# Forming the block sums of the second round's left operands at the transposes, and keeping them in DRAM

## The chip, the core and the metric

The kernel runs on one core of one Trainium2 chip. The core has a matrix engine (TensorE, PE in the profile, with PEld for its weight loads), VectorE (DVE), ScalarE (ACT), GpSimd (POOL), and SyncE (SP), whose queue issues all DMAs of this kernel. The engines run their own instruction queues in order and wait for each other by semaphores. The metric is the time on the device, in microseconds, from the median of several runs; lower is better. Before the change it is 2823.95 us, the median of three runs between 2823.14 and 2828.58.

## What is computed

Two layers of a decoder over 2048 positions of width 1024, all in float32. The first ("even") layer has eight dense attention heads, the second ("odd") layer three groups of dilated sliding windows. The change touches the second layer's way in:

```python
def odd_layer(x, g_norm, w_in, g_q, g_k, w_out):
    h = rmsnorm(x, g_norm)
    proj = h @ w_in                       # (2048 x 1024) @ (1024 x 5120)
    q, k, v, gate = jnp.split(proj, split_points(ODD_SIZES), axis=-1)
    ...
    q = rmsnorm(groups(q), g_q)
    k = rmsnorm(groups(k), g_k)
    att = dilated_window_attention(q, k, groups(v))
    mixed = merge_heads(att) * jax.nn.silu(gate)
    return x + mixed @ w_out
```

Here x is the output of the first layer, which ends with its own product, `x + mixed @ w_out`.

## The kernel before

**Products.** A float32 product is made of three TensorE passes over operands split in a high and a low part (`split`, lines 73 to 86: ACT writes the high part, DVE or POOL the rest; `mm3`, lines 88 to 93). A panel is 1024 rows by 512 columns of a result. It is computed by Winograd's form of Strassen's method (`panel_steps`, lines 261 to 339) with seven products of half-size blocks in place of eight. The left side, 1024 rows by 1024, falls into L11, L12, L21 and L22, and the seven left operands are

    A11 = L11   A12 = L12   A22 = L22
    S1 = L21 + L22   S2 = S1 - L11   S3 = L11 - L21   S4 = L12 - S2

A product takes two halves of 24 matmuls each, and after each half the panel calls `tick` (line 292), which lets other work issue a step. A panel thus has 14 of these half products. The products come in the order of line 177, A11, S2, A12, S3, S1, A22, S4. Results leave PSUM through four "res" buffers. For q and k columns each result is squared, summed and scaled (`norms`, lines 117 to 125; lines 1014 to 1020), and every square takes a buffer of the tag "c", of which there are four.

**Rounds.** Each layer's way in runs in two rounds of 1024 rows. A round of the second layer has ten panels: q, k and v of each of three groups, and the gate at the end. The first two panels of a round are opened together (`two`, lines 958 to 969): both do A11 and A12 first, then the rest of one, then of the other. Seven left operands fill seven of the eight "big" buffers, so those of the next round can only be written one by one, as the last panel of the round, the gate panel, gives up its own. `panel` calls `after` behind each product for that, which advances `left(k, T, 1, B, False)` (lines 342 to 419, called at line 1187).

**Left operands.** The rows of the second layer's input x1 lie in DRAM. `transpose_to` (lines 153 to 163) takes a tile of 128 rows: load, norm, eight transposes on TensorE, ACT copies with the gain into two "c" buffers named te, and two stores of 256 KB into T (hT1 in DRAM, hT in the profile), which holds all 2048 columns. `staggered` keeps several tiles in flight. At line 990 the pace of these steps for the second round's rows is set to every fourth half product, and they run beside the first three panels of the first round; `tick.finish()` behind the third panel (line 1208) does what is left.

At the change of rounds `left` then loads blocks of T into "c" buffers (lp), 28 loads of 256 KB, some blocks twice or three times, forms S2, S3, S1 and S4 on DVE and POOL (the helper at line 345), S2, S3 and S4 partly out of the split A11, A12 and S2, and splits each result into the big buffers. The reader finds this arithmetic in the profile as L345, the splits as L81 (ACT) and L86 (DVE), the loads of lp as SPq L362.

**What runs beside it.** Attention units of the second layer are issued step by step by `beat` (lines 1192 to 1197), beginning behind the first v panel. A unit loads q, k and v, transposes on TensorE, and passes through ACT and DVE several times (L1122, L1128, L1137, L1149, L1154). Its buffers "ld", "q" and "pT" are two each; its rows use the tag "x" (three buffers), which the tiles xt of the transposes use too.

**Order.** The program is issued through a scheduler that orders each engine's queue by the order in which the program was written, the free buffers of each tag, and its own model of the durations. So a step that is issued at a later half product has a lower priority there, and a tag without a free buffer holds back whatever needs it.

Of the kernel before, what the change touches and what calls it, by code (L numbers as in the profile page):

```python
# [8 lines left out]
F32 = mybir.dt.float32  # L9
F32R = mybir.dt.float32r  # L10
BF = mybir.dt.bfloat16  # L11
AF = mybir.ActivationFunctionType  # L12
OP = mybir.AluOpType
# [4 lines left out]
P = 128  # L18
S = 2048
D = 1024  # L20
KT = D // P  # L21
CH = 512  # L22
# [14 lines left out]
class K:  # L37
# [114 lines left out]

    def transpose_to(self, T, src, t, gain):

        nc = self.nc
        x = self.w4([P, D], name="xt")
        nc.sync.dma_start(x, src[t * P:(t + 1) * P, :])
        yield
        self.normalise(x)
        yield  # L160
        self.transposed(x, gain, lambda z: self.c2([P, 4, P], name="te"),
                        lambda z, d: nc.sync.dma_start(T[:, z * 4:(z + 1) * 4, t * P:(t + 1) * P], d))

# [12 lines left out]
A11, A12, S2, S3, S1, A22, S4 = range(7)  # L176
ORDER = (A11, S2, A12, S3, S1, A22, S4)
FIRST = (A11, A12, S2, S3, S1, A22, S4)
# [77 lines left out]
def panel(*args, **kw):  # L256
    for _ in panel_steps(*args, **kw):
        pass
# [82 lines left out]

def left(k, T, r, A, staged=True):

    nc = k.nc
    tt = lambda o, a, b, op, e=None: (e or nc.vector).tensor_tensor(o, a, b, op=op)  # L345
    sub, plus = OP.subtract, OP.add

    A.extend([None] * 7)

    def new(j, name):  # L350
        A[j] = k.big([P, 4, 2, CH], F32R, name=name)
        return A[j]

    def put(t, kk, src):
        k.split(t[:, kk, 0], t[:, kk, 1], src, "act", "dve")

    tags = itertools.cycle(("ld", "q", "pT") if staged else ("c",))

    def piece(block, kk):
        c = k.c2(name="lp", tag=next(tags))  # L360
        t0 = r * ROUND + block * CH
        nc.sync.dma_start(c, T[:, kk, t0:t0 + CH])  # L362
        return c

    half = lambda t, kk: [t[:, kk, z].bitcast(F32) for z in range(2)]
    if staged:
        F = k.big([P, KT, CH], name="stage")
        for z in range(2):
            nc.sync.dma_start(F[:, z * 4:(z + 1) * 4], T[:, z * 4:(z + 1) * 4, r * ROUND:r * ROUND + CH])
    for z, name in enumerate(("A11", "A12")):  # L370
        t = new((A11, A12)[z], name)
        for kk in range(4):
            put(t, kk, F[:, z * 4 + kk] if staged else piece(0, z * 4 + kk))
        yield
    t = new(S2, "S2")
    for kk in range(4):
        l21, s = piece(1, kk), piece(1, 4 + kk)
        tt(s, l21, s, plus, nc.gpsimd if kk % 2 else None)
        if staged:
            tt(s, s, F[:, kk], sub)  # L380
            tt(F[:, 4 + kk], F[:, 4 + kk], s, sub, nc.gpsimd)
            tt(F[:, kk], F[:, kk], l21, sub, nc.gpsimd if kk % 2 else None)
        else:
            for h in half(A[A11], kk):
                tt(s, s, h, sub)
        put(t, kk, s)
    yield
    t = new(S3, "S3")
    for kk in range(4):
        if staged:  # L390
            s = F[:, kk]
        else:
            s = piece(1, kk)
            hi, lo = half(A[A11], kk)
            tt(s, hi, s, sub)
            tt(s, s, lo, plus)
        put(t, kk, s)
    yield
    yield
    t, t2 = new(S1, "S1"), new(A22, "A22")  # L400
    for kk in range(4):
        l21, s = piece(1, kk), piece(1, 4 + kk)
        tt(l21, l21, s, plus, nc.gpsimd if kk % 2 else None)
        put(t, kk, l21)
        put(t2, kk, s)
    yield
    t = new(S4, "S4")
    for kk in range(4):
        if staged:
            s = F[:, 4 + kk]  # L410
        else:
            s = k.c2(name="lp")
            hi, lo = half(A[A12], kk)
            h2, l2 = half(A[S2], kk)
            tt(s, hi, h2, sub)
            tt(s, s, lo, plus)
            tt(s, s, l2, sub)
        put(t, kk, s)
    yield


def left_direct(k, x, gain, A, spare):
# [171 lines left out]
def staggered(gens):  # L594

    gens, flight = iter(gens), []
    while True:
        flight = [g for g in flight if next(g, "end") != "end"]
        g = next(gens, None)
        if g is not None:  # L600
            next(g)
            flight.insert(0, g)
        elif not flight:
            return
        yield


def even_projection(k, x, w, first, first_left, early, late):
    tc, nc = k.tc, k.nc
    c2, dr = k.c2, k.dram  # L610
    k.fT = {n: dr.tile([P, 4, 2, S], F32R, name=f"f{n}T") for n in "qk"}
    k.sT = {n: dr.tile([P, 4, 2, S], F32R, name=f"s{n}T") for n in "qk"}
# [154 lines left out]
def even_attention(k, tail):  # L767
# [20 lines left out]
    def load_q(kind, h, u):  # L788
# [7 lines left out]
        return q  # L796

    def qk(kind, h, u, q, tile, left):

        kt, vt = heads[kind, h]  # L800
# [130 lines left out]
def odd_layer(k, x, x1, even_w_out, w_in, w_out, out):  # L931
    tc, nc = k.tc, k.nc
    c2, dr = k.c2, k.dram
    T = dr.tile([P, KT, S], F32, name="hT1")
    plain = lambda c0: [[(c0, 256)], [(c0 + 256, 256)]]
    outs = [(even_w_out, plain(n * CH)) for n in range(2)]
    rounds = [[(n, g) for g in gs for n in "qkv"] + [("gate", 0)] for gs in ((1, 0, 2), (2, 1, 0))]
# [2 lines left out]
                [2, 2] + [2, 1, 1, 1, 1, 1, 1, 1, 1] * 2)  # L940
    A = []
    lefts = left(k, k.mixT, 0, A)
    yield W, lefts

    tick = Pace()

    def residual(r, n):
        def emit(block, half, g, src):
            t0 = r * ROUND + block * CH + g * 256
            c0 = n * CH + half * 256  # L950
            view = lambda d: d[t0:t0 + 256, c0:c0 + 256].rearrange("(r p) c -> p r c", p=P)
            a = c2([P, 2, 256], name="x1t")
            nc.sync.dma_start(a, view(x))
            nc.vector.tensor_tensor(a, src.rearrange("p (r c) -> p r c", r=2), a, op=OP.add)
            nc.sync.dma_start(view(x1), a)
        return each(emit)

    def two(A, emits, tick, after=None):

        ps = [panel_steps(k, A, W, "t", emit, tick, after if n else None, first=("u", "x")[n])  # L960
              for n, emit in enumerate(emits)]
        for p in ps:
            next(p)
        yield
        for p in ps:
            next(p, None)
            yield

    for r in range(2):
        B = []  # L970
        nxt = left(k, k.mixT, 1, B) if r == 0 else left(k, T, 0, B)
        if r == 0:
            pace = Pace()
            pace.every = 2
            pace.add(lefts)
        both = two(A, [residual(r, n) for n in range(2)], pace if r == 0 else tick,
                   lambda j: None if j in EARLY else next(nxt))
        next(both)
        if r == 0:
            pace.finish()  # L980
            next(nxt)
            next(nxt)
        next(both)
        if r == 1:
            tick.finish()
            next(nxt)
            next(nxt)
        next(both)
        A = B
        tick.every = 1 if r == 0 else 4  # L990
        tick.add(iter("-"), staggered([k.transpose_to(T, x1, r * 8 + t, k.go) for t in (4, 5, 6, 7, 0, 1, 2, 3)]))

    qk = [dr.tile([S, 2, 2, HW], F32, name=f"qk{g}") for g in range(3)]
    vv = [dr.tile([S, 2, HW], F32, name=f"vv{g}") for g in range(3)]
# [189 lines left out]

    for r in range(2):
        B = []
        nxt = left(k, T, 1, B, False)
        for i, (name, grp) in enumerate(rounds[r]):
            rate = 3 if r == 0 or i < 3 else 1.3
            count = [0.0]  # L1190

            def beat():
                tick()
                count[0] += 1
                if count[0] >= rate:
                    count[0] -= rate
                    step()

            last = r == 0 and name == "gate"
            if i < 2:  # L1200
                if i == 0:
                    both = two(A, [emitter(r, *rounds[r][n]) for n in range(2)], beat)
                    next(both)
                next(both)
            else:
                panel(k, A, W, "t", emitter(r, name, grp), beat, (lambda j: next(nxt)) if last else None)
            if r == 0 and i == 2:
                tick.finish()
            if name == "v":
                nblk = S // GROUPS[grp][1] // P  # L1210
                if nblk == 1:
                    if r == 1:
                        queue.extend((True, attention(grp, hf, range(16), range(1))) for hf in range(2))
                else:
                    ns = range(r * nblk // 2, (r + 1) * nblk // 2)
                    queue.extend((False, attention(grp, hf, range(GROUPS[grp][1]), ns)) for hf in range(2))
        A = B
    ws = []
    for n in range(2):
        t = k.big([P, 4, 2, CH], F32R, name="wof")  # L1220
# [126 lines left out]
```

## Time and profile before

| | |
|---|---|
| median of three runs | 2823.95 us |
| profiled execution, its own time | 2826.53 us |
| its span, first to last instruction | 2824.8 us |
| busy share PE / DVE / ACT / POOL | 95% / 73% / 57% / 43% |
| mean granted TensorE clock | 0.979 |
| DMA moved | 449.43 MB, mean 159 GB/s |

The span is the profiled execution's time on the core; its own time is 1.7 us more, and 2.6 us above the median of the runs. A busy PE is not PE at its peak, since the ends of matmuls are modelled; the number of PE instructions in a stretch tells more. In lines of single instructions the columns are start, duration, engine, line, operation, what is written and read, and in square brackets the idle time before it and what ended that. In lines of groups the numbers are busy time and mean ns of one, then the idle time before them.

### The profile page before, as it was taken

Reading aid. Unit: us, or ns where it says so; the run is one execution under the profiler, and the core shown is the slowest. Engines: PE = TensorE matmul, PEld = TensorE weight load, DVE = VectorE, ACT = ScalarE, POOL = GpSimd, SP = SyncE. Lnnn points to the kernel's source line nnn. Section 1 sums busy time; section 2 is a strip of 40 time slices with the busy share of each in tenths; the row PEclk is TensorE's granted clock in tenths of the full one; section 3 lists DMA queues with packets and bytes.
Section 4 is the critical chain, followed back from the end, with each engine's and each line's share of the span. In section 5 each row is a group of like instructions: output and inputs, shape, how many; then the busy total and the mean of one; then the engine's idle time right before and its main releaser. Section 6 shows DMA issues by size and latency. Waiting matters only on the chain.

```text
span 2824.8 us, 55621 instructions
## 1 busy us (share of the span) xinstructions
PE 2676.4 (95%) x20191; PEld 2455.5 (87%) x20191; DVE 2052.7 (73%) x4373; ACT 1618.6 (57%) x3924; POOL 1223.4 (43%) x981
## 2 busy tenths in 40 slices
PE   6999999999999999998987999999989999999998
PEld 5898878998787789987887999999889999999876
DVE  7857684684888888888959857476797686763966
ACT  6465553454776666665364555555664577665642
POOL 3545464544544433326545544343245432422322
PEclk9999999999999999999998999999999999999999
DMA  5576544445433344435577553334543445444675
GB/s 180 181 222 210 172 160 154 154 142 192 144 111 118 112 123 144 139 104 173 187 232 246 154 179 107 121 122 146 169 128 126 139 140 166 132 147 134 219 254 183
DMA packets 398770, 449.43 MB, mean 159 GB/s; under 512 B 31712, under 2 KB 331040, under 8 KB 398496
## 3 DMA queue, kind: packets, MB, share of 16 engines
q1 hardware_dynamic: 398496, 445.89, 49.4%
q8 instruction: 159, 2.61, 0.4%
q14 instruction: 115, 0.94, 0.1%
HBM read 291.22 MB, written 154.57 MB: 158 GB/s over the span
## 4 chain that ended last, share of the span: by engine, by line
PE 62%; DVE 21%; DMA 7%; ACT 5%; issue 3%; POOL 1%; SPq 1%; DVEq 0%; ACTq 0%; POOLq 0%
PE ps L91 17%; PE ps L93 17%; PE ps L92 17%; DVE rest L828 4%; PE ps L863 2%; PE ps L1145 2%; DVE wop L86 2%; DVE A L86 2%; PE ps L1135 2%; PE ps L1116 2%; DVE lp L345 1%; DVE S L86 1%; PE ps L1061 1%; DVE pT L86 1%; DVE c L300 1%
## 5 line engine op out<-in xcount | busy, mean ns | idle before, releaser
L226 POOL TENSOR_TENSOR wraw<-wraw 128x512 f32<-128x512 f32 (+1 forms) x320 | 444.2, 1400 | 430.3 <-DVE wop L86 157.1
L81 ACT ACTIVATE wop<-wraw 128x512 fp32r<-128x512 f32 (+1 forms) x560 | 349.5, 629 | 383.4 <-PE ps L93 294.2
L86 POOL TENSOR_TENSOR wop<-wraw,wop 128x512 fp32r<-128x512 f32 (+1 forms) x240 | 329.4, 1375 | 534.0 <-ACT wop L81 503.8
L92 PE MATMUL ps<-wop,S 128*128 128x256 f32 (+1 forms) x1792 | 512.4, 286 | 18.1 <-DVE wop L86 16.8
L91 PE MATMUL ps<-wop,A 128*128 128x256 f32 (+1 forms) x1792 | 512.0, 287 | 14.2 <-DVE c L300 13.5
L91 PE MATMUL ps<-wop,S 128*128 128x256 f32 (+1 forms) x1792 | 515.8, 289 | 9.9 <-DVE c L300 6.3
L92 PE MATMUL ps<-wop,A 128*128 128x256 f32 (+1 forms) x1792 | 511.7, 286 | 2.2 <-DVE wop L86 1.5
L93 PE MATMUL ps<-wop,S 128*128 128x256 f32 (+1 forms) x1792 | 512.9, 287 | 0.0
L93 PE MATMUL ps<-wop,A 128*128 128x256 f32 (+1 forms) x1792 | 509.5, 285 | 0.0
L86 DVE TENSOR_TENSOR wop<-wraw,wop 128x512 fp32r<-128x512 f32 (+1 forms) x320 | 270.2, 845 | 232.0 <-ACT wop L81 230.6
L92 PEld LDWEIGHTS ps<-wop,S 128*128 128x128 f32 x1792 | 343.3, 192 | 21.0 <-DVE wop L86 17.8
L91 PEld LDWEIGHTS ps<-wop,A 128*128 128x128 f32 x1792 | 342.3, 191 | 19.0 <-issue 13.4
L91 PEld LDWEIGHTS ps<-wop,S 128*128 128x128 f32 x1792 | 342.1, 191 | 15.1 <-issue 8.4
L92 PEld LDWEIGHTS ps<-wop,A 128*128 128x128 f32 x1792 | 342.9, 191 | 4.0 <-DVE wop L86 3.2
L93 PEld LDWEIGHTS ps<-wop,S 128*128 128x128 f32 x1792 | 342.7, 191 | 3.3 <-issue 2.6
L93 PEld LDWEIGHTS ps<-wop,A 128*128 128x128 f32 x1792 | 342.7, 191 | 1.4 <-issue 0.8
L300 DVE TENSOR_TENSOR c<-u,ps 128x512 f32<-128x512 f32 (+1 forms) x274 | 178.7, 659 | 91.9 <-PE ps L93 86.1
L81 ACT ACTIVATE pT<-ps 128x512 fp32r<-128x512 f32 (+2 forms) x352 | 165.5, 504 | 135.6 <-PE ps L863 81.3
L831 POOL TENSOR_TENSOR rows<-rows,rest 128x512 f32<-128x512 f32 (+4 forms) x160 | 152.6, 957 | 162.1 <-DVE rest L828 141.8
L86 DVE TENSOR_TENSOR pT<-ps,pT 128x512 fp32r<-128x512 f32 (+2 forms) x352 | 188.0, 559 | 44.2 <-ACT pT L81 42.8
L1128 ACT ACTIVATE row<-row,nm 128x256 f32<-128x256 f32 (+1 forms) x384 | 172.5, 452 | 64.4 <-DVE nm L1126 63.9
L92 PE MATMUL ps<-pT,vt 128*128 128x256 f32 x576 | 171.1, 299 | 5.5 <-DVE pT L86 5.3
(214 smaller groups left out, 6485.0 us busy)
## 6 DMA issues: line engine op xcount, KB each, us to landing
wraw<-in_odd_w_in_dram SPq DMA_DIRECT2D x88, 512.0 KB, 4.0
wraw<-in_even_w_in_dram SPq DMA_DIRECT2D x70, 512.0 KB, 4.2
ld<-qk SPq DMA_DIRECT2D x106, 256.0 KB, 3.2
qk<-c SPq DMA_DIRECT2D x96, 256.0 KB, 2.4
lp<-hT SPq DMA_DIRECT2D x60, 256.0 KB, 3.6
uu<-ot SPq DMA_DIRECT2D x96, 132.0 KB, 1.9
fin<-uu SPq DMA_DIRECT2D x16, 792.0 KB, 4.5
hT<-te SPq DMA_DIRECT2D x48, 256.0 KB, 4.3
```

The source lines that it names most:

```text
L81: nc.scalar.activation(hi, src, AF.Copy)
L86: (nc.vector if lo_on == "dve" else nc.gpsimd).tensor_tensor(lo, src, hi.bitcast(F32), op=OP.subtract)
L91: mm(out, a[0], b[0], start=start, stop=False, skip_group_check=more)
L92: mm(out, a[0], b[1], start=False, stop=False, skip_group_check=more)
L93: mm(out, a[1], b[0], start=False, stop=stop, skip_group_check=more)
L226: tt = lambda e, o, x, y, op, s: e.tensor_tensor(o[:, s], x[:, s], y[:, s], op=op)
L300: nc.vector.tensor_tensor(out[g], x[g], y[g], op=OP.add)
L828: nc.vector.tensor_tensor_scan(o[:, b:b + n][:, ::-1], back, k.ident[:, :1].to_broadcast([P, n]), 1.0 if carry is None else carry, OP.mult ...
L831: nc.gpsimd.tensor_tensor(dst[:, :w], dst[:, :w], o[:, b + 1:b + 1 + w], op=OP.mult)
L863: nc.tensor.transpose(pt[:, (jx * 2 + i) * P:(jx * 2 + i + 1) * P], rows[:, i, (jj * 2 + jx) * P:(jj * 2 + jx + 1) * P], k.ident)
L1116: nc.tensor.matmul(scores(hp, e), q[pr, za, hp], ring[pr, zb, hp, blocks], start=i == 0, stop=i == 2)
L1128: nc.scalar.activation(row[:, h // 2, h % 2, :nk], row[:, h // 2, h % 2, :nk], AF.Exp, bias=nm[:, h:h + 1], accum_out=ot[:, HW + HG + h:HW ...
```

## The change

For the second round's rows of the second layer, a new generator `combined_to` takes the place of `transpose_to`. It takes a pair of tiles, ta of the upper block row and tb of the lower (8 + i and 12 + i, for i from 0 to 3). Each pair has six steps: both loads, a norm, a norm, the transposes of ta, those of tb, and then the sums. Four transposed halves a0, a1, b0, b1 (parts of L11, L12, L21, L22) stay in the four "c" buffers until the sums are made: S1 and S3 on POOL, S2 and S4 on DVE, in buffers of the tags "ld", "q" and "pT" and, for S3, in place. All seven operands go to a new DRAM tensor U (hU1), 7 stores of 256 KB for each pair. T keeps only the first round's 1024 columns.

The pairs run one behind the other, a step every third half product, and `tick.finish()` moves from behind the third to behind the seventh panel. At the change of rounds `left_ready` loads each operand's four blocks (28 loads of 256 KB in all) and splits them, one operand behind each of the gate panel's seven products; nothing is added or subtracted there.

```diff
+def combined_to(U, k, src, ta, tb, i, gain):
+    nc = k.nc
+    xs = {}
+    for t in (ta, tb):
+        xs[t] = k.w4([P, D], name="xt")
+        nc.sync.dma_start(xs[t], src[t * P:(t + 1) * P, :])
+    yield
+    for t in (ta, tb):
+        k.normalise(xs[t])
+        yield
+    got = {}
+
+    def store(j, d):
+        nc.sync.dma_start(U[:, j, :, i * P:(i + 1) * P], d)
+
+    tags = {(ta, 0): "c", (ta, 1): "c", (tb, 0): "c", (tb, 1): "c"}
+    for t in (ta, tb):
+        k.transposed(xs[t], gain, lambda z: got.setdefault((t, z), k.c2([P, 4, P], name="te", tag=tags[t, z])))
+        yield
+    a0, a1, b0, b1 = got[ta, 0], got[ta, 1], got[tb, 0], got[tb, 1]
+    store(A11, a0)
+    store(A12, a1)
+    store(A22, b1)
+    s1, s2, s4 = (k.c2([P, 4, P], name="lp", tag=n) for n in ("ld", "q", "pT"))
+    nc.gpsimd.tensor_tensor(s1, b0, b1, op=OP.add)
+    store(S1, s1)
+    nc.vector.tensor_tensor(s2, s1, a0, op=OP.subtract)
+    store(S2, s2)
+    nc.gpsimd.tensor_tensor(b0, a0, b0, op=OP.subtract)
+    store(S3, b0)
+    nc.vector.tensor_tensor(s4, a1, s2, op=OP.subtract)
+    store(S4, s4)
+    yield
+
+
+def left_ready(k, U, A):
+    A.extend([None] * 7)
+    for j in FIRST:
+        t = A[j] = k.big([P, 4, 2, CH], F32R, name=f"A{j}")
+        for kk in range(4):
+            c = k.c2(name="lp")
+            k.nc.sync.dma_start(c, U[:, j, kk])
+            k.split(t[:, kk, 0], t[:, kk, 1], c, "act", "dve")
+        yield
...
-    T = dr.tile([P, KT, S], F32, name="hT1")
+    T = dr.tile([P, KT, S // 2], F32, name="hT1")
+    U = dr.tile([P, 7, 4, CH], F32, name="hU1")
...
-        tick.every = 1 if r == 0 else 4
-        tick.add(iter("-"), staggered([k.transpose_to(T, x1, r * 8 + t, k.go) for t in (4, 5, 6, 7, 0, 1, 2, 3)]))
+        tick.every = 1 if r == 0 else 3
+        if r == 0:
+            tick.add(iter("-"), staggered([k.transpose_to(T, x1, t, k.go) for t in (4, 5, 6, 7, 0, 1, 2, 3)]))
+        else:
+            tick.add(iter("-"), *[combined_to(U, k, x1, 8 + i, 12 + i, i, k.go) for i in range(4)])
...
-        nxt = left(k, T, 1, B, False)
+        nxt = left_ready(k, U, B)
...
-            if r == 0 and i == 2:
+            if r == 0 and i == 6:
                 tick.finish()
```

## The prediction

> **What bounds the kernel now.** I read the page first, then busy time by stretches around the two places that the change touches, then the instructions of each engine in order of time where TensorE loses time.
>
> ```profile
> span 2824.8 us, 55621 instructions
> PE 2676.4 (95%) x20191; PEld 2455.5 (87%) x20191; DVE 2052.7 (73%) x4373; ACT 1618.6 (57%) x3924; POOL 1223.4 (43%) x981
> PE 62%; DVE 21%; DMA 7%; ACT 5%; issue 3%; POOL 1%; SPq 1%; DVEq 0%; ACTq 0%; POOLq 0%
> ```
>
> TensorE is the bound. Other engines cost time only where TensorE stands still, and a busy share of 95% does not show how much that is, so I count its instructions per stretch. The change of rounds (the gate panel of the first round and the start of the second) lies between 1990 and 2140 us. Columns: start and end, length, then busy time and number of instructions of PE, PEld, DVE, ACT, POOL, then granted clock, DMA share, GB/s.
>
> ```profile
> 2000.00:2020.00 20.00, 20.00 (x181) 18.41 (x180) 15.21 (x31) 13.76 (x35) 4.28 (x4) 1.00 0.71 224
> 2020.00:2040.00 20.00, 16.81 (x126) 14.97 (x127) 16.13 (x34) 11.69 (x30) 2.56 (x2) 0.83 0.56 165
> 2040.00:2060.00 20.00, 20.00 (x181) 19.26 (x178) 17.09 (x33) 15.81 (x36) 5.58 (x4) 1.00 0.70 221
> 2060.00:2080.00 20.00, 14.06 (x112) 12.68 (x111) 18.68 (x33) 12.67 (x31) 11.91 (x7) 0.81 0.31 100
> 2080.00:2100.00 20.00, 20.00 (x173) 18.78 (x173) 19.27 (x38) 14.15 (x36) 7.99 (x6) 0.93 0.27 77
> 2100.00:2120.00 20.00, 18.73 (x169) 17.20 (x168) 18.63 (x38) 10.58 (x33) 10.53 (x8) 1.00 0.39 129
> 2120.00:2140.00 20.00, 18.73 (x169) 17.15 (x169) 18.50 (x43) 10.96 (x28) 13.86 (x10) 1.00 0.29 98
> 2570.00:2625.00 55.00, 55.00 (x485) 51.20 (x486) 25.67 (x74) 30.36 (x81) 16.63 (x14) 1.00 0.44 142
> ```
>
> Undisturbed, PE starts 181 instructions in 20 us (9.05 per us). The second stretch lacks 55 of them: 55/9.05 = 6.1 us lost. The fourth and fifth lack 69 and 8: 8.5 us. The sixth and seventh lack 24: 2.7 us. The last row is a stretch of attention without any left operands to form: PE loses nothing there, with DVE at 26 of 55 us. So the change of rounds holds **14.6 us** in two stalls, and 2.7 us more behind them. What is at their heads:
>
> ```profile
> 2021.54 1.29 POOL L345 TENSOR_TENSOR lp<-lp 128x512 f32<-128x512 f32 x1 [6.53 <-DMA lp<-hT]
> 2022.86 1.79 DVE L345 TENSOR_TENSOR lp<-lp,A 128x512 f32<-128x512 f32 x1 [3.56 <-POOL lp L345]
> 2025.07 0.63 ACT L1011 ACTIVATE e<-e 128x512 f32<-128x512 f32 x1 [4.03 <-POOL wop L86]
> 2028.59 1.11 PE L1135 MATMUL ps<-ident,row 128*128 128x128 f32 x4 [3.19 <-ACT pT L1137]
> ...
> 2066.56 1.77 DVE L345 TENSOR_TENSOR lp<-A,S 128x512 f32<-128x512 f32 x1 [1.18 <-POOL lp L345]
> 2068.37 1.65 DVE L345 TENSOR_TENSOR lp<-lp,A 128x512 f32<-128x512 f32 x1
> 2070.05 1.64 DVE L345 TENSOR_TENSOR lp<-lp,S 128x512 f32<-128x512 f32 x1
> 2071.73 0.63 ACT L81 ACTIVATE S<-lp 128x512 fp32r<-128x512 f32 x1 [2.62 <-DVE lp L345]
> 2073.72 1.11 PE L1135 MATMUL ps<-ident,row 128*128 128x128 f32 x4 [3.37 <-ACT uT L1149]
> 2077.41 0.58 PE L91 MATMUL ps<-wop,A 128*128 128x256 f32 x1 [2.57 <-DVE c L300]
> ```
>
> First stall: the add of a left block on POOL (L345 is the arithmetic of `left`) stands 6.5 us for a load of hT, holding the split of a weight behind it on POOL and the next sum on DVE; ACT waits 4.0 us for them and reaches the attention's evacuation (pT) late; PE waits 3.2 us for that. Second stall: three sums of S4 in a row, each over 1.6 us, hold DVE; ACT waits 2.6 us for their split, is late at uT, and DVE is late at the partial result c. In both, left-operand arithmetic is in the queue ahead of what PE needs.
>
> **The change, part by part.**
>
> *Removed at the change of rounds.*
>
> ```profile
> L345 DVE TENSOR_TENSOR lp<-lp,A 128x512 f32<-128x512 f32 x16 | 15.1, 942 | 5.1 <-POOL lp L345 4.9
> L345 POOL TENSOR_TENSOR lp<-lp 128x512 f32<-128x512 f32 x4 | 5.4, 1346 | 10.9 <-DMA lp<-hT 7.6 <-DVE lp L345 3.4
> L345 DVE TENSOR_TENSOR lp<-A,S 128x512 f32<-128x512 f32 x4 | 3.8, 959 | 1.2 <-POOL lp L345 1.2
> L345 DVE TENSOR_TENSOR lp<-lp,S 128x512 f32<-128x512 f32 x4 | 3.7, 922 | 0.0
> L345 DVE TENSOR_TENSOR lp<-lp 128x512 f32<-128x512 f32 x4 | 3.3, 831 | 2.4 <-DMA lp<-hT 2.4
> L345 DVE TENSOR_TENSOR lp<-A,lp 128x512 f32<-128x512 f32 x4 | 2.7, 686 | 0.9 <-DMA lp<-hT 0.9
> L81 ACT ACTIVATE A<-lp 128x512 fp32r<-128x512 f32 x12 | 6.9, 622 | 3.4 <-DMA lp<-hT 3.4
> ```
>
> All of L345 goes: 32 DVE instructions, 28.6 us, and 4 on POOL, 5.4 us. In 2000 to 2100 DVE is busy 86.4 us of 100 by the rows above; it falls to about 58, toward the 47% of the quiet stretch. The 28 loads stay 28 (7 operands of 4 blocks, where `left` read some blocks twice), of the same 256 KB, and the 28 splits stay. But now every split is the first to touch a load: ACT waits for DMA itself. Today it does so for 12 splits at 3.4 us in all, so 28 make about 8 us of ACT waits, in pieces that mostly lie under PE's own work. Bounds: nothing left of the stalls (14.6 us gained), or the first stall stays because ACT now stands where POOL stood (8.5 gained). I take 3 us left over, half of the first stall, since the ACT waits seen so far are short: **-11.6 us**. The 2.7 us behind the second stall belong to the norms of the first panels, where no lp instruction is left: 0, with -2.7 as the far end.
>
> On the price of a stall, the row at 2020 shows the granted clock at 0.83 although PE stood only 3.2 us, and that the loss by count (6.1 us) is twice the gap. [...]
>
> *Added in the first six panels.* Four times two POOL and two DVE sums, twelve more stores of 256 KB (28 for 16), and the same loads, norms, transposes and ACT copies as before, later. A step comes every third half product instead of every fourth, 25 steps, two tiles in six steps. A half product is 24 matmuls, and the 341 instructions of the quiet row below in 40 us make it 2.8 us, so a step is 8.4 us, the last half product with a step is the 75th, and the work that ended at 1665 us now runs on to about 1800 (42 half products to some 1674, then 33 at an estimated 3.8 us: the six panels with attention between there and the gate panel near 1995 take some 53 us each, in 14 half products).
>
> ```profile
> 1540.00:1560.00 20.00, 15.02 (x113) 14.61 (x112) 18.79 (x31) 7.86 (x19) 16.33 (x12) 0.83 0.31 109
> 1580.00:1600.00 20.00, 14.88 (x106) 14.67 (x106) 16.52 (x27) 9.37 (x25) 11.96 (x9) 0.83 0.50 157
> 1620.00:1660.00 40.00, 40.00 (x341) 40.00 (x341) 23.50 (x52) 27.89 (x72) 17.37 (x13) 1.00 0.74 226
> 1700.00:1740.00 40.00, 37.22 (x321) 34.98 (x318) 29.10 (x69) 21.39 (x62) 21.39 (x16) 0.96 0.30 98
> 1780.00:1820.00 40.00, 40.00 (x358) 37.56 (x359) 15.96 (x49) 21.32 (x64) 11.20 (x9) 1.00 0.48 154
> L162 SPq DMA_DIRECT2D hT<-te x16: 359/372/1136, 1573.0 to 1665.1; - x16
> SPq L1022 <- POOL c L1020: 31.1, 10, 11.7
> ```
>
> The eight new DVE sums cost 8 x 0.69 = 5.5 us if alone and 8 x 1.77 = 14 us at worst, the eight on POOL 8 x 1.35 = 10.8 us, the twelve stores 12 x 0.37 = 4.4 us of SP's queue. Over 260 us this is under a tenth of each, and DVE is 40 to 73% busy from 1620 on with PE full: hidden, if it falls there. Should that cover be gone, the 14 us of DVE would be paid. The moved ACT work (half of 64 copies, norms of four tiles) lands in stretches where ACT is 53 to 70% busy: hidden too. What is not hidden is where they stand in a queue. The first pair's transposes and sums fall near 1585 to 1605, where PE already loses: 106 instructions for 170 (341 in 40 us), 7.5 us. There, before, a norm and a tile came every step; after, two tiles in six, so a little less DVE work, and then the sums. Ends: this stall goes (-7.5) or a second of its kind appears (+7.5). I take **+3 us**, nearer to a loss, because SP already waits 31.1 us on POOL for results to store, and the block sums add POOL work and stores to that queue.
>
> The row at 2022.86 against the 0.69 us of the same sums elsewhere shows what a POOL sum does to a DVE sum beside it. [...]
>
> *Sum.* -11.6 + 3 = -8.6 us. The profiled execution has its own time of 2826.5 us, 2.6 us above the median of 2823.95; on it the change makes 2817.9, and on the median **2815.4 us**, rounded to 2815.5.
>
> **Rivals.**
>
> *A. The loads take the stalls' place.* The splits wait for loads that wait for buffers: SP is held up for DVE's splits today.
>
> ```profile
> SPq L362 <- DVE S L86: 14.7, 5, 7.6
> SPq L362 <- DVE A L86: 13.8, 6, 6.4
> ```
>
> 28.5 us of SP's time go to loads of left blocks that wait for one of the four "c" buffers, with the attention's loads queued behind. The tag stays "c" and now every block passes through it. If one stall remains whole and half the other, the change of rounds gains 14.6 - 6.1 - 4.2 = 4.3, and with +3 for the panels the time is 2824 - 1.3 = 2822.7. Against it: the splits that free the buffers come sooner without 28.6 us of sums between them.
>
> *B. Slower: the four "c" buffers in the panels.* A pair keeps all four as its transposed blocks, from the second tile's transposes until the sums are made and stored. The squares of the q and k norms need the same tag. The pairs' second transposes fall at half products 18, 36, 54 and 72 of panels 0 (q), 2 (v), 3 (q) and 5 (v, just behind k's last result); three of the four meet results of q or k. Results can wait in four "res" buffers, two results deep, so it decides from the point where the hold outlasts the gap to the third result, some 11 us (two products). The hold: eight copies 3 us, four sums 4 us, a store 4 us, together 11 us if nothing else delays them, so it is at the edge.
>
> ```profile
> L149 ACT ACTIVATE te<-ps,go x64: 347/373/411, 1571.9 to 1664.6; 128x128 f32<-128x128 f32 x64
> hT<-te SPq DMA_DIRECT2D x48, 256.0 KB, 4.3
> ```
>
> Each such stall costs what 1580 to 1600 shows, 7.5 us; three of them make 22.5, and with -11.6 the time is 2824 + 10.9 = 2834.9. Two make 2827.4. Against it: the results in question are the last of a panel, and the next panel's first result comes three products later.
>
> *C. More gained.* Panels 0 to 2 get lighter, since half of the tiles leave them, and the stall at 1580 goes too: -14.6 - 7.5 and no +3, 2801.9; with half of that stall left, 2805.6.
>
> *D. It does not do what it says*: the stalls are the attention's own chain of small steps meeting the gate's exponentials, and other work stands in the queue in place of the sums. Then 0 to +3, 2824 to 2827. Against it is the quiet row at 2570, which has the attention without a stall.
>
> **How the numbers follow.** Forecast 0.48 (own range 2810 to 2821), A 0.18, B 0.17, C 0.11, D 0.06. A change of under 0.2% (5.6 us, so 2818.3 to 2829.6) can't be told from none. Faster: all of C, 0.42 of the forecast's 0.48, 0.04 of A: 0.57. Same: 0.06 of the forecast, 0.14 of A, 0.05 of D and a bit of B: 0.26. Slower: most of B and a bit of D: 0.17. The range leaves out C's far end and B's three stalls: 2804 to 2831.
>
> **What would show it.** Right: no L345 in the change of rounds; DVE near 60 us of 100 there; PE back to about 181 per 20 us at 2020 to 2100 (shifted by what comes before), granted clock 1.00. The panel term: PE counts at 1540 to 1620 unchanged within 40, those from 1700 on full. Wrong: PE waits of 3 us for ACT that waits for DMA lp (A); squares or c waiting for stores of te and lp, with counts of 110 per 20 us at 1600, 1720 or 1790 (B). Most of all the forecast fails if the order of the work around 1540 to 1820 falls out otherwise than I think, since that term is small only as long as nothing there becomes late.

## The result, and the profile after

The changed kernel takes 2804.99 us (median of 4 runs, 2800.0 to 2807.47) against 2826.26 us for the kernel before in runs beside it: a ratio of **0.9923**, with a 95% interval of 0.9903 to 0.9943, so 0.6 to 1.0% faster. The forecast was 2815.5 us, a gain of 0.3%; the sign and the range held, the size was under half of what came, and the median lies 1.0 us inside the lower end of the range. Three executions in the whole study, two of the kernel before and the profiled one of the version for the first layer alone, ran at a mean granted clock of 0.56 to 0.77 and took 3140 to 4222 us; they are left out of all that follows.

The page of the profile after, whose own time is 2807.47 us (span, busy shares, chain of waits):

```profile
span 2805.7 us, 55659 instructions
PE 2667.5 (95%) x20191; PEld 2448.1 (87%) x20191; DVE 2021.5 (72%) x4349; ACT 1617.4 (58%) x3924; POOL 1229.9 (44%) x985
PE 67%; DVE 18%; DMA 5%; ACT 5%; issue 3%; POOL 1%; SPq 1%; DVEq 0%; ACTq 0%; POOLq 0%
```

DVE has 24 instructions fewer (32 sums gone, 8 come) and POOL four more, as counted. DVE's part of the chain falls from 21% to 18%, and PE's rises from 62% to 67%. The same stretches of the change of rounds as before, in the same columns:

```profile
2000.00:2020.00 20.00, 20.00 (x181) 18.61 (x182) 13.50 (x28) 16.85 (x40) 4.45 (x3) 1.00 0.74 237
2020.00:2040.00 20.00, 20.00 (x182) 18.68 (x181) 17.31 (x44) 16.66 (x43) 1.46 (x1) 1.00 0.80 249
2040.00:2060.00 20.00, 20.00 (x178) 19.10 (x178) 15.49 (x32) 18.55 (x44) 6.48 (x5) 1.00 0.60 201
2060.00:2080.00 20.00, 19.85 (x180) 18.37 (x178) 15.23 (x34) 11.66 (x34) 13.67 (x11) 1.00 0.37 113
2080.00:2100.00 20.00, 19.71 (x176) 17.95 (x175) 11.65 (x33) 12.29 (x33) 8.07 (x6) 1.00 0.34 114
2100.00:2120.00 20.00, 19.56 (x181) 18.00 (x181) 18.22 (x45) 11.05 (x30) 12.90 (x10) 1.00 0.22 74
2120.00:2140.00 20.00, 20.00 (x181) 19.53 (x178) 12.39 (x25) 8.78 (x24) 9.53 (x7) 1.00 0.52 168
```

No stretch lacks more than 5 of 181 PE instructions, and the granted clock is 1.00 in all of them; both stalls and the slow stretch behind them are gone. DVE is busy 73.2 us of 100 between 2000 and 2100, not near 60. What is left of the left operands there are the 28 splits, with what they waited for (groups of the stretch 1970 to 2095, then a row each of all engines' waits and of SP's waits, 1985 to 2100):

```profile
L86 DVE TENSOR_TENSOR A<-lp,A 128x512 fp32r<-128x512 f32 x28 | 19.8, 735 | 12.2 <-ACT A L81 12.2
L81 ACT ACTIVATE A<-lp 128x512 fp32r<-128x512 f32 x28 | 16.4, 626 | 4.5 <-DMA lp<-hU 3.6 <-PE ps L93 0.8
```

```profile
ACT A L81 <- DMA lp<-hU: 3.6, 5, 1.1
```

```profile
SPq L466 <- DVE A L86: 21.4, 12, 6.4
```

ACT waits 3.6 us for loads, in five pieces, none over 1.1 us. SP still stands 21.4 us for the "c" buffers, without harm to PE: between 2000 and 2140 its only waits are 0.4 us for ACT's pT and 0.3 us for DVE's ot.

To see where the 19 us of the span went I compare the start of the same PE instruction in two traces; every kernel here has 20191 of them. Four marks are enough: instruction 9609 (at 1519 us in the trace before), 13597 (1999 us, ahead of the first stall), 14690 (2139 us) and the last. The differences from one mark to the next are what each stage gained (minus) or lost, in us:

```
                          to 9609   panels 0 to 8   change of rounds   rest    span
                                    (to 13597)      (to 14690)
changed kernel              3.2        -4.3             -16.8          -1.2   -19.1
```

The change of rounds carries nearly all of it. In the panels one step stands out, at 1580 to 1600, where PE's count is 137 instead of 106: 5.1 us gained, 1.7 of them lost again. The 3.2 us ahead of 1519 are small shifts at places that the change doesn't touch. They also tell how far a stage can be trusted, since each is read from one execution: in the changed kernel and the nine versions below that keep the first layer as it was, this stage moves by -1.4 to +4.3 us, and the profiled execution lies up to 6.4 us from the median of its runs (8.0 us in the version for both layers). The rows of the panels in the changed kernel:

```profile
1540.00:1560.00 20.00, 15.02 (x111) 14.61 (x110) 18.47 (x27) 10.10 (x24) 18.16 (x14) 0.83 0.40 135
1580.00:1600.00 20.00, 17.45 (x137) 17.24 (x136) 18.92 (x25) 8.04 (x20) 17.24 (x13) 0.91 0.33 98
1620.00:1660.00 40.00, 40.00 (x341) 40.00 (x340) 26.62 (x52) 22.12 (x52) 19.36 (x15) 1.00 0.68 215
1700.00:1740.00 40.00, 37.28 (x327) 35.36 (x327) 31.99 (x84) 26.64 (x74) 25.13 (x18) 1.00 0.50 159
1780.00:1820.00 40.00, 40.00 (x359) 37.56 (x359) 16.18 (x49) 19.41 (x54) 12.11 (x10) 1.00 0.59 181
```

### The profile page after: what moved, and what is told of

Same layout as the page of the kernel before. It is cut to its first block, busy times and chain, and to the rows that moved or that the text cites. A ratio compares the mean times of both kernels' runs of the same rounds, so it can differ in the third digit from the quotient of the medians.

```text
span 2805.7 us, 55659 instructions
## 1 busy us (share of the span) xinstructions
PE 2667.5 (95%) x20191; PEld 2448.1 (87%) x20191; DVE 2021.5 (72%) x4349; ACT 1617.4 (58%) x3924; POOL 1229.9 (44%) x985
## 4 chain that ended last, share of the span: by engine, by line
PE 67%; DVE 18%; DMA 5%; ACT 5%; issue 3%; POOL 1%; SPq 1%; DVEq 0%; ACTq 0%; POOLq 0%
PE ps L91 18%; PE ps L92 18%; PE ps L93 18%; DVE rest L877 4%; PE ps L912 3%; PE ps L1198 3%; PE ps L1188 2%; PE ps L1169 2%; DVE A L86 2%; PE ps L1114 2%; DVE wop L86 1%; DVE pT L86 1%; DVE S L86 1%; DVE c L300 1%; PE ps L1161 1%
## 5 line engine op out<-in xcount | busy, mean ns | idle before, releaser
L91 PE MATMUL ps<-wop,A 128*128 128x256 f32 (+1 forms) x2432 | 695.6, 287 | 14.3 <-DVE c L300 13.4
L92 PE MATMUL ps<-wop,A 128*128 128x256 f32 (+1 forms) x2432 | 694.0, 286 | 1.9 <-DVE wop L86 1.6
L93 PE MATMUL ps<-wop,A 128*128 128x256 f32 (+1 forms) x2432 | 691.8, 285 | 0.0
L91 PEld LDWEIGHTS ps<-wop,A 128*128 128x128 f32 x2432 | 462.2, 190 | 20.0 <-issue 16.6
L92 PEld LDWEIGHTS ps<-wop,A 128*128 128x128 f32 x2432 | 462.6, 190 | 5.4 <-DVE wop L86 2.9
L93 PEld LDWEIGHTS ps<-wop,A 128*128 128x128 f32 x2432 | 462.3, 190 | 2.4 <-issue 1.2
L92 PE MATMUL ps<-wop,S 128*128 128x256 f32 (+1 forms) x1152 | 329.1, 286 | 17.1 <-DVE wop L86 17.0
L91 PE MATMUL ps<-wop,S 128*128 128x256 f32 (+1 forms) x1152 | 331.7, 289 | 8.0 <-DVE c L300 3.5
L93 PE MATMUL ps<-wop,S 128*128 128x256 f32 (+1 forms) x1152 | 328.7, 286 | 0.0
L92 PEld LDWEIGHTS ps<-wop,S 128*128 128x128 f32 x1152 | 222.0, 193 | 18.8 <-DVE wop L86 18.2
L91 PEld LDWEIGHTS ps<-wop,S 128*128 128x128 f32 x1152 | 220.8, 192 | 12.6 <-DVE c L300 4.1
L93 PEld LDWEIGHTS ps<-wop,S 128*128 128x128 f32 x1152 | 221.5, 192 | 1.5 <-issue 1.5
```

Source lines behind the costliest of these rows:

```text
L91: mm(out, a[0], b[0], start=start, stop=False, skip_group_check=more)
L92: mm(out, a[0], b[1], start=False, stop=False, skip_group_check=more)
L93: mm(out, a[1], b[0], start=False, stop=stop, skip_group_check=more)
```

## The experiments

The theory: the gain is the block arithmetic that no longer stands ahead of PE's feeders at the change of rounds. Its rivals: the gain comes from moving the transposes (or from another order of the queues that comes with it); it comes from loading and deriving the operands differently, not from the sums; and, for the panels, that the "c" buffers' hold has a price that the chosen pace happens to avoid. All ratios are against the kernel before, run on the same chip, with 95% intervals.

### Moving the transposes without the sums

```diff
 (kernel before)
-        tick.every = 1 if r == 0 else 4
+        tick.every = 1 if r == 0 else 7
-            if r == 0 and i == 2:
+            if r == 0 and i == 6:
```

> The kernel before, with nothing changed but the pace: the transposes of the second round's rows spread over six panels (a step every seventh half product) and finished behind the seventh. Theory 1 (the gain is the block arithmetic that no longer stands in the queues at the change of rounds): the change of rounds keeps its loss of 14 to 17 us and its L345 rows, the panels move by 3 us either way; 2826 us, between 2821 and 2830. Theory 2 (the gain comes from taking the transposes out of the first panels, and another order of the queues): at least half of the gain appears here, 2805 to 2816.

Measured: 2830.47 us, ratio 1.0019 (1.001 to 1.0029). It is 0.2% slower, so at this pace the gain does not come from where the transposes lie. By stages: panels +5.1 us, change of rounds +1.7 us. The loss stays there, in other pieces: its stretches from 2020 to 2100 have 159, 156, 138 and 133 PE instructions. The panels' loss, and the time by half a microsecond, lie outside what theory 1 allowed (3 us, and 2821 to 2830), on the side away from theory 2.

### The arithmetic put back, on one engine and on both

In the changed kernel, between the load and the split of each block, as many idle operations as the kernel before had sums in that operand (the three versions in one, shortened):

```diff
             k.nc.sync.dma_start(c, U[:, j, kk])
+            again = {S2: 3, S3: 2, S1: 1, S4: 3}.get(j, 0)
+            for n in range(again):
+                on_pool = n == 0 and j in (S2, S1) and kk % 2
+                if on_pool:      # left out in the DVE version
+                    v = c.rearrange("p (a b) -> p a b", b=HD)
+                    k.nc.gpsimd.tensor_tensor(v, v, k.zero.unsqueeze(1).to_broadcast([P, CH // HD, HD]), op=OP.add)
+                else:            # left out in the POOL version
+                    k.nc.vector.tensor_tensor(c, c, c, op=OP.max)
             k.split(t[:, kk, 0], t[:, kk, 1], c, "act", "dve")
```

> The changed kernel with 32 idle DVE instructions (the larger of a block and itself, 128x512) put between the loads and the splits, where the kernel before had its 32 DVE sums; POOL's four sums stay away, the result is unchanged. Theory 1a (DVE's time in the queue is the price): most of the gain at the change of rounds is lost, 2814 to 2822. Theory 1b (the waits between POOL, DMA and DVE are the price, DVE has room): under a quarter is lost, 2804 to 2809.

> The changed kernel with only POOL's four sums put back (a block plus a row of zeros, which changes nothing), each between a load and its split. Theory 1a: 2804 to 2808. Theory 1b: the stall behind POOL's wait for a load returns, 6 us or more of the gain are lost, 2810 to 2816.

> Both put back: 32 idle DVE instructions and four on POOL at the change of rounds, beside the sums at the transposes. If the arithmetic at the change of rounds is the whole of the gain, it is lost: 2819 to 2828, with PE counts near 110 to 130 in 20 us somewhere between 2020 and 2100. If a part of the gain came from the operands no longer being built out of each other and out of blocks loaded twice, 2810 to 2817.

```
                 median us   ratio (95% interval)       change of rounds   panels 0 to 8   span
changed kernel    2804.99    0.9923 (0.9903, 0.9943)         -16.8             -4.3        -19.1
DVE's 32 back     2819.6     0.9985 (0.9974, 0.9996)          -5.8             -4.9         -8.8
POOL's 4 back     2811.16    0.9952 (0.9934, 0.997)          -12.8             -1.3        -17.3
all 36 back       2824.96    1.0000 (0.999, 1.0009)           -0.3             -1.0         -3.9
```

With all of it back the gain is gone, in the median and in the stage. The idle operations are much the same load as the sums: DVE's 32 take 31.3 us there, where the sums took 28.6. So the sums are the whole of it; that the operands are no longer built from each other, or that no block is loaded twice, is worth nothing visible (the interval is some 3 us either way). DVE's sums cost 16.8 - 5.8 = 11.0 us, POOL's four 16.8 - 12.8 = 4.0 us, together 15.0 where both make 16.5. Neither 1a nor 1b alone is right: the price lies mostly in DVE's queue, and four POOL sums cost a quarter of it by the stage (by the ratios 0.29%, some 8 us, with intervals of 5 us either way). What each brings back, from the stretches of the POOL version, of the DVE version (two rows) and of the version with both (four rows):

```profile
2040.00:2060.00 20.00, 16.81 (x138) 15.77 (x137) 14.62 (x30) 17.37 (x44) 5.55 (x5) 0.93 0.55 173
```

```profile
2020.00:2040.00 20.00, 17.52 (x145) 16.50 (x144) 17.79 (x45) 11.85 (x32) 0.73 (x1) 0.91 0.69 214
2060.00:2080.00 20.00, 17.88 (x145) 16.77 (x144) 20.00 (x31) 10.55 (x21) 14.63 (x9) 0.91 0.27 81
```

```profile
2020.00:2040.00 20.00, 18.46 (x163) 16.99 (x162) 17.97 (x35) 13.21 (x33) 2.89 (x2) 1.00 0.68 216
2040.00:2060.00 20.00, 17.96 (x157) 16.70 (x157) 16.58 (x42) 17.01 (x40) 5.28 (x4) 1.00 0.65 200
2060.00:2080.00 20.00, 17.17 (x143) 15.88 (x141) 19.25 (x30) 12.42 (x30) 11.83 (x9) 0.91 0.39 119
2080.00:2100.00 20.00, 16.68 (x144) 15.20 (x144) 18.85 (x39) 13.31 (x40) 7.88 (x6) 1.00 0.36 114
```

POOL's sums make one stall of 43 instructions, some 4.8 us at 9.05 per us. DVE's make two of 36, and the two stretches behind the second lack 21 and 18 more. With both the loss is spread over these four stretches, at a granted clock of 0.91 in the third and 1.00 in the others, though it adds up to the same as the two long stalls of before (607 of 724 instructions over 2020 to 2100, so 117 or some 13 us, against 132 before; with 2100 to 2140 taken in, where 325 of 362 are left, 154 against 156). So the shape of the stalls in the trace before was that of one order of the queues; their sum was not.

### The pace and the place of the pairs

Five versions of the changed kernel leave the change of rounds alone and change only when the pairs are issued in the panels.

```diff
 every second half product:   -tick.every = 1 if r == 0 else 3    +tick.every = 1 if r == 0 else 2
 longer hold:    +    yield
                 +    yield
                      a0, a1, b0, b1 = got[ta, 0], got[ta, 1], got[tb, 0], got[tb, 1]
 later:               xs = {}
                 +    yield
                 +    yield
                      for t in (ta, tb):
 sums at once:        k.transposed(...)
                 -    yield
                 +    if t == ta:
                 +        yield
 pair at once:        k.transposed(...)
                 -    yield
```

> The changed kernel with a step every second half product: the four pairs finish at half product 50 instead of 75, two of them inside the first two panels where VectorE is fullest. If the panels carry a cost of crowding that the chosen pace holds down (rival B, the four c buffers and the queues), it is slower than the change, 2808 to 2816; if the panels take the pairs for nothing at any pace, 2803 to 2807.

> The changed kernel with two empty steps between a pair's transposes and its sums, so that the four c buffers are meant to be held for six half products more (some 17 us) and the sums stand lower in the order. Rival B (the norms of q and k wait for c and TensorE stops): two or three stalls of 7 us, 2815 to 2828. If the hold does not reach TensorE: 2803 to 2808.

> The changed kernel with two empty steps ahead of a pair's loads, not between its transposes and its sums: the work reaches as far into the attention's panels as in the run with the longer hold (99 half products), but the four c buffers are meant to be held no longer than in the change. If the hold of c (rival B) made that run lose 22 us: 2803 to 2810. If it is the meeting with the attention units (their rows share the tag of the tiles xt, and PSUM's t banks are shared): 2815 to 2830.

> The changed kernel without the step between the second tile's transposes and the sums: five steps for a pair, 21 in all, done at half product 63, and the c buffers held three half products less. If the hold or the meeting with the attention still costs something in the change: 2796 to 2803. If neither does, or the sums now meet fuller queues: 2803 to 2810.

> The changed kernel with both tiles' transposes and the sums in a single step: four steps for a pair, 17 in all, done at half product 51, before the attention units are many. Shortest hold, but bursts of 16 transposes and 16 copies. Less meeting with the attention: 2794 to 2803. Bursts that crowd the first panels as the pace of every second half product did: 2808 to 2820.

```
                    median us   ratio (95% interval)      panels 0 to 8   change of rounds
changed kernel       2804.99    0.9923 (0.9903, 0.9943)       -4.3            -16.8
sums at once         2807.48    0.9927 (0.9909, 0.9945)       -2.3            -16.3
every second         2818.8     0.9969 (0.996, 0.9978)         7.5            -16.1
later                2818.53    0.9969 (0.9959, 0.9978)       10.7            -16.0
pair at once         2824.49    0.999  (0.9981, 1.0)           6.9            -16.1
longer hold          2828.96    1.0007 (0.9998, 1.0017)       17.2            -16.9
```

"Sums at once" came out as expected where the step costs nothing; every second, the longer hold and the pair at once were slower than the slower of the two cases written down. The gain at the change of rounds is the same to within a microsecond in all of them. What decides the result is the other term, and it runs from a gain of 4 us to a loss of 17. ("Pair at once" also lost 4.3 us ahead of 1519 and 7.2 us behind 2139.) The longer hold takes back the whole gain. Two stretches of it with the attention running and a shorter one out of the second, then who waited for te in 1740 to 1960, and PE's longest waits in 1540 to 2000:

```profile
1780.00:1820.00 40.00, 35.75 (x297) 32.11 (x296) 25.25 (x83) 26.16 (x75) 5.79 (x5) 0.96 0.65 208
1860.00:1900.00 40.00, 37.81 (x303) 33.12 (x302) 26.52 (x76) 21.99 (x67) 17.74 (x13) 0.85 0.45 138
1888.00:1905.00 17.00, 16.19 (x89) 13.80 (x90) 14.47 (x48) 11.14 (x40) 6.25 (x4) 0.50 0.50 156
```

```profile
  ACT sq L123: 3.2, 3
```

```profile
PE ps L1190 <- DVE box L86: 4.7, 1, 4.7
PE ps L91 <- DVE c L300: 3.1, 1, 3.1
PE ps L92 <- DVE wop L86: 3.1, 1, 3.1
PE ps L1208 <- DVE ot L1177: 3.0, 2, 1.6
```

In the first of the two PE has 297 instructions where the changed kernel has 359. The squares do wait for the held buffers, 3.2 us in three waits, which they never do in the changed kernel (there one step of a norm waits 4.9 us for them, once, between 1540 and 1960). But the waits of PE that are longer than in the changed kernel are those for the attention's small steps (box 4.7 us, where the changed kernel has 2.3), and all of PE's waits in 1540 to 2000 come to 19.5 us against 12.7, which is only a third of the 21.5 us between the two kernels. By estimate the clock has the larger share. Between 1888 and 1905 it is at 0.50, and PE starts 89 instructions where 154 are usual, 7.2 us lost, although PE's waits from 1880 to 1910 are four, the longest 1.4 us. From 1519 to 2000 the clock records show 41 us at half in this run against 17 us in the changed kernel; at the rate of that stretch (7.2 us lost in 17) the 24 us more cost some 10 us, an estimate. "Later", which is written with no longer hold, loses 10.7 us in the panels as well, with 36 us at half clock. So the hold alone isn't the cause; the place matters too. What makes the attention's small steps late is open: the rows of an attention unit and the tiles xt share buffers, and each edit gives all queues another order. The runs that crowd the pairs lose in other places again. "Pair at once", with 16 transposes and four sums in a step, loses in the first panels, where DVE is fullest. Its stretch 1580 to 1620, and PE's longest wait in 1540 to 1760:

```profile
1580.00:1620.00 40.00, 31.13 (x243) 30.96 (x242) 34.28 (x60) 16.92 (x37) 27.94 (x20) 0.87 0.36 110
```

```profile
PE ps L91 <- DVE u L300: 8.9, 1, 8.9
```

### The same treatment in other places

```diff
 (first layer's change of rounds)
-        nxt = left(k, T, 1, B)
+        nxt = left_ready(k, U, B)
-  tick.add(staggered(k.transpose_to(T, x, t, k.ge) for t in range(TPC * 2, NTT)))
+  tick.add(*[combined_to(U, k, x, 8 + i, 12 + i, i, k.ge) for i in range(4)])
 ...
 (second layer's first round, in the version for both)
-        ... else left(k, T, 0, B)
+        ... else left_ready(k, U0, B)
```

> The changed kernel with the same treatment at the two other places where left operands come from transposed rows: the first layer's change of rounds (a loss of some 9 us at 360 to 400) and the second layer's first round (16 us at 1500 to 1540). If the gain is the arithmetic taken out of the queues at the change, both places gain: 2785 to 2798. In the second place there are only 28 half products for 25 steps, so the sums stand as near to the change as before; if that decides, it gains nothing there: 2796 to 2806.

> The changed kernel with the same treatment at the first layer's change of rounds alone, where the transposes have four panels: the 9 us at 360 to 400 mostly go, 2796 to 2802. If the price there is the three-fold splits' own time (VectorE and ScalarE) and not the sums, 2802 to 2808.

> The changed kernel with the sums in the step of the second tile's transposes, and the same treatment at the first layer's change of rounds. The trace of the version for both layers shows some 9 us gained at 360 to 400 and about half of it given back at 480 to 700 by another order of the queues. If the sums' earlier place keeps the gain: 2793 to 2802. If the order behind it takes it back as it did with the pairs in six steps: 2803 to 2812.

For both places: 2825.79 us, ratio 0.9997 (0.9986 to 1.0008). By stages, 7.6 us gained up to 1519 and 22.6 us lost in the panels, 19.3 us of it in the work that the kernel before does between 1530 and 1540. In this place the loads do take the place of the sums, as rival A has it. A stretch of this run (the kernel before has 147 PE instructions in it, with DVE busy all 20 us), and two waits, the first from 1495 to 1560, the second from 1515 to 1570:

```profile
1520.00:1540.00 20.00, 7.42 (x48) 7.21 (x48) 14.70 (x15) 10.57 (x18) 9.18 (x6) 0.71 0.63 198
ACT A L81 <- DMA lp<-hU: 32.2, 15, 6.2
PE ps L91 <- DVE c L300: 17.7, 2, 13.6
```

ACT's splits wait 32.2 us for the loads, where they waited 3.6 us at the change of rounds, DVE's half of the splits waits for ACT, and the partial results that PE needs (c) stand behind it. Four "c" buffers pass all 28 loads, and SP waits 15.9 us in 17 pieces for the splits that free them. For the first layer alone: 2805.89 us, ratio 0.9928 (0.9911 to 0.9944), nothing beyond the change; no stages are given for it. With the sums moved into the step of the second tile's transposes as well: **2796.58 us, ratio 0.9894 (0.9878 to 0.9911)**, the fastest of the study, 1.1% under the kernel before. Its interval and that of the change overlap by a little, so that it beats the change rests on medians 8 us apart in different sets of runs. By stages it has -13.3 us ahead of 1519, -2.2 in the panels and -15.8 at the change of rounds.

Where it gained is not where I had expected. I had read a gain of 9 us at 360 to 400 out of the version for both layers; that was a stall moved by 20 us. In the fastest version, too, the first layer's change of rounds keeps its stall; 9.0 us are gained by 280, and 6.7 of them come at 240 to 280, where the first layer's transposes run. The kernel before, then this version:

```profile
240.00:260.00 20.00, 16.77 (x138) 15.91 (x137) 19.86 (x33) 9.24 (x18) 9.93 (x7) 1.00 0.70 235
260.00:280.00 20.00, 17.44 (x136) 16.95 (x136) 17.54 (x27) 8.85 (x19) 8.27 (x7) 0.91 0.38 124
360.00:380.00 20.00, 15.38 (x55) 11.70 (x54) 20.00 (x18) 8.00 (x15) 14.78 (x11) 0.83 0.55 171
380.00:400.00 20.00, 18.79 (x78) 14.16 (x78) 19.27 (x23) 13.97 (x24) 10.50 (x9) 1.00 0.46 158
```

```profile
240.00:260.00 20.00, 18.89 (x160) 18.46 (x159) 18.14 (x33) 12.42 (x28) 11.65 (x9) 1.00 0.54 167
260.00:280.00 20.00, 20.00 (x171) 19.85 (x171) 16.52 (x33) 14.00 (x34) 11.65 (x16) 1.00 0.81 250
360.00:380.00 20.00, 18.69 (x76) 13.70 (x75) 16.83 (x20) 10.61 (x20) 9.37 (x6) 1.00 0.74 246
380.00:400.00 20.00, 16.83 (x64) 12.68 (x63) 9.21 (x13) 12.56 (x21) 10.77 (x9) 0.91 0.38 119
```

From 240 to 280 PE has 331 instructions instead of 274. From 360 to 400 it has 140 instead of 133, of 176 in an undisturbed stretch, although DVE is busy 26 us there instead of 39. ACT's splits wait there for loads again, 11.4 us in eight waits between 355 and 400, and PE waits 2.5 us for ACT; whether that is what holds it was not tested.

## Why the prediction was right, and where it was short

**What bounds the kernel there.** Right. PE lost time at the change of rounds to left-operand arithmetic in the queues ahead of its feeders; the version with all 36 operations back has the time of the kernel before, ratio 1.0000. The sign that DVE would be busy near 60 us of 100 did not come: it is 73.2 us, since other work moves up into the stretch when PE doesn't stand (897 PE instructions in the five rows from 2000 to 2100, after 773). The two stalls that I counted to 14.6 us were real as a sum, but their heads were not causes that can be taken one by one: with POOL's wait gone and DVE's sums left, PE still loses 11 us.

**The term at the change of rounds** was put at -11.6 us and measured -16.8: this is the step that was short. Two parts of it were mis-sized. First, 3 us were kept back for ACT's waits for loads, estimated at 8 us; they were 3.6 us over the 28 splits, and none reached PE. Second, the 2.7 us behind the stalls were put at 0, as belonging to the norms of the first panels; they went too (362 PE instructions in 2100 to 2140, after 338), and came back with the sums (325 with all 36 operations back). The far end that I named for both, 14.6 + 2.7 = 17.3, is what nearly came.

**The term of the panels**, +3 us, came out at -4.3 from mark to mark, 1.1 us better than before by 1999 with the 3.2 us of small shifts ahead of 1519, which is within what a stage moves by itself. The stall at 1580 eased (137 instructions for 106) where I had leaned to a second one. The eight DVE sums took 10.7 us, between the 5.5 and 14 us that I had given: four took 6.5 us, the other four 4.2. (The DVE sum of 1.79 us at 2022.86 in the trace before has POOL's split of a weight beside it, 1.32 us from 2022.79 on, and not the POOL sum, which had ended at 2022.83; the DVE sum at 2009.67, with no POOL instruction beside it, took 0.69 us. Whether POOL is the cause was not tested.) That the eight sums, at these times, and the twelve stores are hidden held at the chosen pace; the five versions show that this is a property of the pace and not of the work, for the same work cost 7 to 17 us at four other paces or places and nothing at one.

**The sum.** -8.6 was forecast and -19.1 measured between the two profiled spans, 1.2 us of it behind 2139 (-21.3 between the medians). That the time still fell into the range, 2804 to 2831, by 1.0 us, is partly luck: both terms erred to the same side, and the forecast's own range began at 2810. The price of a stall was rightly taken by PE's count and not by the gap: PE's three waits, 3.2 + 3.4 + 2.6 = 9.2 us, less the 3 us kept back, would have given 6.2 us of gain at that place.

**Rivals.** A, loads in place of the sums: fell for the change, by ACT's 3.6 us and SP's 21.4 us that no PE instruction waited for. It came true in the version for both layers, with 32.2 us of ACT's waits. B, the "c" buffers: did not happen in the change, and something of its size happened in the run with the longer hold, which lost 21.5 us in the panels against the change, near the 22.5 us of B's three stalls, and ended at 2829, within the 2827 to 2835 that I had worked out. That is luck in the number: its path as I told it, squares waiting for "c", is only 3.2 us of the waits there. By the estimate above the larger part went by PE's waits, 19.5 us against 12.7 and longer at the attention's small steps, and by the clock, 41 us at half against 17; what makes those steps late is open. C, more gained, was the nearest in time: 2801.9 to 2805.6 against 2804.99, by the stalls gone whole and the stall at 1580 eased. It had a chance of 0.11. D fell with the runs that put the arithmetic back.

## What to carry to other kernels

Where the engine that bounds a kernel loses time at a hand-over, look at what stands in the queues of its feeders there, and move that arithmetic to where the same data pass anyway; put the operations back as idle ones to learn whether they were the cause. Count the bound engine's instructions by stage: the gain of the moved work and the price of where it was moved to then show separately, and here the first was constant at 16 us while the second ran from -4 to +17 us with the pace and place alone. So a change of this kind should be run at a few paces before it is judged. And where loads take the place of arithmetic, look at each place for what waits for them: 3.6 us and no harm at one hand-over, 32.2 us and a loss at another.

## What the runs showed of the hardware that was not expected

The granted clock fell below 1.00 beside short waits of PE. In the run with POOL's sums back, PE's longest wait in the change of rounds is 2.6 us, and the clock of the stretches that follow is 0.66 and 0.91 (waits of PE in 2000 to 2140, then stretches of 4 us):

```profile
PE ps L1198 <- DVE ot L1185: 2.6, 1, 2.6
```

```profile
2052.00:2056.00 4.00, 1.36 (x12) 1.15 (x12) 3.55 (x12) 3.36 (x8) 1.27 (x1) 1.00 0.89 308
2056.00:2060.00 4.00, 3.45 (x23) 2.91 (x22) 3.12 (x8) 4.00 (x13) 1.70 (x2) 0.66 0.38 131
2060.00:2064.00 4.00, 4.00 (x33) 4.00 (x33) 2.47 (x3) 3.81 (x9) 4.00 (x3) 0.91 0.15 52
```

The counts of 12, 23 and 33 where 36 are usual make 40 instructions lost, 4.4 us for a wait of 2.6. The stretch of 4 us with a third of its usual instructions still has a clock of 1.00; the two behind it have 0.66 and 0.91. In the run with the longer hold the clock stayed at 0.50 for 17 us with no wait over 1.4 us beside it. The version with both put back lost 117 instructions over four stretches with its clock at 1.00 in three of them, so a loss is not told by the clock alone.
